# Hybrid decoder block on one core: the second half of the tokens gathered in three 8-bit parts for the first pair of experts, and the sorting of the experts behind it

## The chip, the cores and the metric

The kernel runs on one NeuronCore of one Trainium2 chip. The metric is the time of one execution on the device in microseconds (us). The kernel before takes 444.64 us, the median of 3 runs (443.95 to 445.56).

## What is computed

A decoder block over 272 tokens (16 learned meta tokens and 256 of the input) of width 1024: a normalisation, one projection whose columns feed two mixers (a state-space mixer and a gated short convolution), a product with the output weights, a residual sum, and a mixture of experts, all in float32. The part that the change touches is the last one:

```python
p_group = softmax(t @ wg_r + bg_r)
g_val, g_idx = top_k(p_group, 1)
...
top_v, top_i = top_k(sel, TOP_K)
top_w = softmax(top_v)
...
for e in range(N_EXPERTS):
    h = silu(t @ w_gate[e]) * (t @ w_up[e])
    out = out + combine[:, e:e + 1] * (h @ w_down[e])
```

Each of 256 tokens picks one group of four experts and two experts in it. There are 16 experts, each with three float32 matrices of 1024 x 512, about 100 MB of weights in all.

## The kernel before, in words

**Stages.** The projection, the mixers and the output product fill the first 225 us. Then the router chooses experts, and a loop goes over `UNITS`: six pairs of experts, then one group of four. `side_by_side` puts a pair's two products next to each other in the array, 64 columns each; so a pair can hold at most 64 tokens of each expert, which is checked at the end (`rv > CAP`).

**Tokens to slots.** The tokens lie in `hh`, two halves (b = 0 and 1) of 128 tokens by 1024 values, each row scaled. `rk` holds the rank of a token among those of an expert; `pick` makes of it a 0/1 matrix `P` (token by slot), and a product with `P` gathers an expert's tokens, already turned, into the PSUM tile `xp`. `rows` (VectorE) multiplies `xp` by a column of weights and writes `X`, the moving operand's partner in the products `gu` (gate, then up). For the first pair `gather` (line 900) uses float32 `hh` and float32 `P`. For the later pairs `gather3` (line 1110) uses bf16: each float32 value is split into three bf16 parts of 8 bits each, `hparts[j][b]`, with three products per block and half. The parts are made by ScalarE (`Copy` to bf16) and VectorE (subtraction) after the first `X`, at lines 1099 to 1108, while TensorE does the first pair's `gu`.

**Router and sorting.** `ranks(b)` needs the choice of half b; the second half's ranks also count the first half's tokens. `sort_experts` (line 876, 15 small VectorE instructions) sorts ten of the experts by their number of tokens (the first `FIXED` = 6 stay where they are): `order` says which expert stands at which place, `mosti` is the largest count, `rk` is put in order. `weights` (line 997) makes the tokens' weights of their experts, `cparts`.

**Sequencer numbers.** `values_load` (line 1176) lets every engine's sequencer read `mosti` into a register (`TENSOR_LOAD`), which only the branch at the end needs. Line 1177 lets SyncE's queue (SP) read `order` into ten registers, which the loads of weights of the sorted experts need.

**Weights.** All weights come by DMAs of 1 MB, issued in order by SP (line 113) into a ring of 22 slots plus 3 more (`RING2`), 25 tiles in all. A tile's slot is freed when TensorE has read it (`used`, called after every fourth block of `gu` and every second of `yd`), and the next load into it is issued then. A pair takes 12 tiles: 4 gate, 4 up, 4 down. `fin`, a 512 KB copy of the last normalisation's weights to all partitions, is loaded at line 774, in the middle of the projection.

**A pair.** `gu` gate (8 blocks), `gu` up (8 blocks), then `back` (line 1031: products `ptp` with `P` and `cparts`), `gather3` of the next pair in two pieces with the turning `hbp` of the hidden values between them, then `yd` (down), whose results are scattered to the accumulators `acc` during the next pair's `gu`.

```python
for kind in range(2):
    g = bank("pj", "gu")
    for k in range(KT):
        side_by_side(g, Xf, w_of(u, kind, k, 0, 512), k, k == 0, k == KT - 1)
        if k % 4 == 3:
            used(ne)
```

Of the kernel before, what the change touches and what calls it, by code (L numbers as in the profile page):

```python
# [39 lines left out]
def body(ctx, tc, x, meta_tokens, norm_mix, w_in, ssd_conv_w, ssd_conv_b, dt_bias, A_log, D_skip,  # L40
# [95 lines left out]

    fin = cp.tile([128, D], F32, name="fin")
    lg = cp.tile([128, 2, 20], F32, name="lg")
# [601 lines left out]
    for i, (name, j, c, t0) in enumerate(units):  # L740
        hold(i)
        if name[0] == "c" and c == 0:
            cc = v["cc" + name[1]]
        split_hi(i + 2)
        if i == B + 1:
            split_hi(i + 3)
        for f, a in pre.get(i, []):
            f(*a)
        if name == "o":
            if c == 0:  # L750
                second(i - 1)
            split_lo(i + 2)
            if c < 14:
                for b in range(2):
                    out_product(i, b)
        else:
            p = project(i)
            split_lo(i + 2)
            if i in (0, 1):
                x_part(i, 1 - i)  # L760
            if i == B + 1:
                first(i, p)
            if i:
                second(i - 1)
            if i != B + 1:
                first(i, p)
        fill(i)
        if i == NU - 1 and dbg is not None and "yn" in dbg:
            nc.sync.dma_start(dbg["yn"][:, 0:2048], v["y", 0].rearrange("p t l -> p (t l)"))
        if i == NU - 1:  # L770
            eu.close()
            right = ctx.enter_context(tc.tile_pool(name="ring2", bufs=RING2, side="right"))
            load(RING2, right)
            nc.sync.dma_start(fin, raw(norm_final, 0, [[0, 128], [1, D]]))
    if dbg is not None and "yn" in dbg:
# [73 lines left out]
    def ranks(b):  # L849

        p = rp[:, 64 + 16 * b:80 + 16 * b]
        T.matmul(p, sup, mem[:, b], start=True, stop=(b == 0))
        if b:
            T.matmul(p, onesb, mem[:, 0], start=False, stop=True)
        V.scalar_tensor_tensor(rk[:, b, 0:NE], mem[:, b], -1024.0, p, op0=OP.mult, op1=OP.add)

# [18 lines left out]

    def sort_experts(counts):
        m, key = NE - FIXED, place
        t = small("srt", 2 * m * m)
        c = counts[:, FIXED:NE]
# [20 lines left out]
    def gather(b, q, p, i0=0, i1=4):  # L900

        for i in range(i0, i1):
            T.matmul(p[:, i], hh[:, b].rearrange("p (m k) -> p k m", k=KT)[:, 4 * q + i],  # L903
                     P[:, b], start=(b == 0 and i == 0), stop=(b == 1),
                     skip_group_check=True)

# [55 lines left out]
    busy(1)  # L962
    P = bp.tile([128, 2, 128], F32, name="P")
    pick(P, 0, 0)
# [3 lines left out]
    xp = [bank(tag, "xp").rearrange("p (k t) -> p k t", k=4) for tag in ("pj", "m")]  # L968
    gather(0, 0, xp[0])
    for i in range(4):  # L970
        places(1, i)
    gather(0, 1, xp[1], 0, 1)
    ranks(1)
    gather(0, 1, xp[1], 1, 4)
    pick(P, 0, 1)

# [5 lines left out]
    mosti = cp.tile([128, 1], I32, name="mosti")  # L982
    sort_experts(rp[:, 96:112])
    for q in range(2):
        gather(1, q, xp[q])
    es.close()
# [97 lines left out]

    h3 = wk.tile([128, 2, D], BF, name="h3")
    tm = wk.tile([128, S], F32, name="tm", tag="PT")
    X = wk.tile([128, KT, 128], F32, name="X")
    for q in range(2):
        rows(X, xp[q], q)
    weights(tm)  # L1090
    ws0 = wk.tile([128, 1], F32, name="ws", tag="ws")
    P = wk.tile([128, 2, 128], BF, name="P", bufs=2)
    for b in range(2):
        pick(P, 0, b)


    hb0, hb1 = (hh[:, b].bitcast(BF).rearrange("p (j d) -> p j d", j=2) for b in range(2))
    hparts = [[h3[:, 0], hb0[:, 0]], [h3[:, 1], hb0[:, 1]], [hb1[:, 0], hb1[:, 1]]]
    rem = [wk.tile([128, 512], F32R, name="rem", tag=t).bitcast(BF) for t in ("Yh", "Yl")]
# [29 lines left out]
    def over():  # L1129
# [45 lines left out]

    rv = nc.values_load(mosti[0:1], min_val=0, max_val=2 * S)
    chosen += nc.values_load_multi_w_load_instructions(
        order[0:1], engines=[mybir.EngineType.SP], min_val=FIXED, max_val=NE - 1,
        skip_runtime_bounds_check_because="a sum of one of the numbers FIXED to NE - 1 and of zeros")[1]
    left = {}  # L1180
    s3 = wk.tile([128, 2], F32, name="s3")
    s4 = wk.tile([128, 2, 2], F32, name="s4")
    for u, ne in enumerate(UNITS):
# [19 lines left out]
        if last:  # L1203

            A.activation(s3[:, 0:1], eps, AF.Sqrt)
            hd = turned(hb)
        PT, ws = back(P, cparts[:, :, places_of(u)])
        if not last:
# [105 lines left out]
```

## Time and profile before

| | |
|---|---|
| median of 3 runs | 444.64 us |
| the profiled execution | 445.38 us |
| span of the profiled execution, first to last instruction | 443.4 us |
| TensorE matmul busy | 423.8 us (96%) |
| TensorE weight load busy | 295.0 us (67%) |
| VectorE, ScalarE, GpSimd busy | 220.3, 159.0, 89.1 us |
| mean granted TensorE clock | 0.989 |
| HBM read | 138.26 MB |

Times inside the profile count from the first instruction. PE is TensorE's matmuls and PEld its weight loads, DVE is VectorE, ACT ScalarE, SPq SyncE's queue, which issues the DMAs; PEldq, DVEq and so on are the sequencers. `L1050` is line 1050. In a timeline row stand the start, the time taken, engine, line, operation, the tiles, shapes and a count, and in brackets how long the engine was idle before and who released it. A float32 product of the program shows as two matmul records.

### The profile page before, as it was taken

The page shows a single profiled execution, that of the slowest core. Times are in us where ns is not written, and L with a number is a line of the kernel's source. Part 1 is how long each engine was busy: PE and PEld are TensorE (multiplying, and loading weights), DVE is VectorE, ACT ScalarE, POOL GpSimd, SP SyncE. Part 2 cuts the span into 40 slices and gives each one's busy share as a digit, 9 for nine tenths or more (in the row PEclk, how much of TensorE's full clock was granted, in tenths as well). Part 3 has the DMA queues.
Part 4 walks back from the last instruction along what each step waited for, and adds up shares of the span by engine and source line. Part 5 has one row for each costly group of instructions (what it writes and reads, how often), then busy time and mean ns, then how long its engine had stood idle before and what let it go on. Part 6 is the DMA issues. An engine that isn't in the chain of part 4 may idle for free.

```text
span 443.4 us, 7446 instructions
## 1 busy us (share of the span) xinstructions
PE 423.8 (96%) x2923; PEld 295.0 (67%) x2923; DVE 220.3 (50%) x465; ACT 159.0 (36%) x247; POOL 89.1 (20%) x113
## 2 busy tenths in 40 slices
PE   8899999899999899999999999999999999999982
PEld 5799999799998899888877363533535335353241
DVE  7769888758795768695557521110212102121013
ACT  6766346645757344744472401010010100101121
POOL 2345334854668154000000000000000000000000
PEclk9999999999999999999999989999999999999997
DMA  8997977066699566599692999999999999999952
GB/s 232 342 312 250 348 250 266 32 191 188 194 360 413 182 209 233 199 407 419 199 362 102 370 400 375 425 418 424 419 421 421 422 418 420 421 418 422 412 224 98
DMA packets 48892, 139.85 MB, mean 315 GB/s; under 512 B 6342, under 2 KB 32342, under 8 KB 36822
## 3 DMA queue, kind: packets, MB, share of 16 engines
q1 hardware_dynamic: 47990, 138.22, 82.5%
q10 hardware_dynamic: 864, 1.12, 0.7%
q8 instruction: 25, 0.41, 0.4%
q14 instruction: 13, 0.11, 0.1%
HBM read 138.26 MB, written 1.06 MB: 314 GB/s over the span
## 4 chain that ended last, share of the span: by engine, by line
PE 64%; DVE 7%; ACT 3%; issue 2%; POOL 1%; DVEq 0%; ACTq 0%
PE gu L1050 22%; PE yd L1050 11%; PE acc L347 10%; PE xp L1115 4%; PE p_c L339 3%; PE acc L1071 3%; PE p_h L339 3%; PE p_b L339 3%; ACT f L310 1%; PE hbp L1057 1%; DVE h L619 1%; PE xp L903 1%; DVE f L326 1%; POOL f L324 1%; DVE h L548 1%
## 5 line engine op out<-in xcount | busy, mean ns | idle before, releaser
L1050 PE MATMUL gu<-w,X 128*64 128x512 f32 (+1 forms) x512 | 100.0, 595 | 0.4 <-DVE X L1082 0.4
L324 POOL TENSOR_TENSOR f<-w,f 128x256 fp32r<-128x256 f32 x96 | 82.6, 892 | 87.5 <-ACT f L310 77.7
L310 ACT ACTIVATE f<-w 128x1024 fp32r<-128x1024 f32 x64 | 67.1, 1054 | 35.9 <-POOL f L324 12.6
L1050 PEld LDWEIGHTS gu<-w,X 128*64 128x64 f32 (+1 forms) x512 | 31.3, 130 | 61.2 <-issue 59.5
L326 DVE TENSOR_TENSOR f<-w,f 128x1024 fp32r<-128x1024 f32 x40 | 50.6, 1264 | 17.4 <-ACT f L310 17.4
L1050 PE MATMUL yd<-w,hd 128*64 128x512 f32 (+2 forms) x288 | 50.9, 548 | 0.5 <-DVE hd L1060 0.5
L347 PE MATMUL acc<-f,h 128*128 128x512 f32 x192 | 44.8, 391 | 0.0
L1202 DVE TENSOR_TENSOR hb<-hb,gu 128x512 f32<-128x512 f32 x7 | 4.8, 688 | 74.0 <-PE gu L1050 71.9
L347 PEld LDWEIGHTS acc<-f,h 128*128 128x128 f32 x192 | 35.5, 188 | 7.7 <-issue 0.4
L1065 ACT ACTIVATE Yh<-yd,ws 128x512 fp32r<-128x512 f32 x13 | 8.9, 688 | 79.2 <-PE yd L1050 62.5
L1050 PEld LDWEIGHTS yd<-w,hd 128*64 128x64 f32 (+1 forms) x288 | 16.7, 128 | 29.3 <-issue 25.5
L1066 DVE SCALAR_TENSOR_TENSOR Yl<-yd,ws,Yh 128x512 fp32r<-128x512 f32 x12 | 9.0, 751 | 53.6 <-PE yd L1050 38.5
L1115 PE MATMUL xp<-P,hh 128*128 128x128 bf16 x192 | 20.1, 232 | 0.0
L1115 PEld LDWEIGHTS <-hh 128*128 128x128 bf16 x192 | 18.8, 149 | 1.6 <-issue 1.6
L1115 PE MATMUL xp<-P,h 128*128 128x128 bf16 x96 | 17.7, 235 | 1.6 <-ACT hb L1196 1.6
L339 PE MATMUL p_z<-uh,f 128*128 128x256 f32 x128 | 17.3, 285 | 1.9 <-POOL f L324 1.9
L339 PE MATMUL p_c<-uh,f 128*128 128x258 f32 x128 | 16.8, 283 | 1.3 <-DVE h L607 1.3
L339 PE MATMUL p_xs<-uh,f 128*128 128x272 f32 x128 | 18.0, 292 | 0.0
L1196 ACT ACTIVATE hb<-gu 128x512 f32<-128x512 f32 x7 | 4.2, 594 | 37.0 <-PE gu L1050 37.0
L339 PEld LDWEIGHTS p_z<-uh,f 128*128 128x128 f32 x128 | 15.6, 188 | 2.4 <-POOL f L324 2.3
L339 PE MATMUL p_b<-uh,f 128*128 128x256 f32 x128 | 16.6, 281 | 0.7 <-DVE h L607 0.7
L1042 ACT ACTIVATE PT<-ptp 128x256 fp32r<-128x256 f32 x7 | 2.7, 385 | 39.7 <-PE ptp L1038 39.7
(331 smaller groups left out, 648.5 us busy)
## 6 DMA issues: line engine op xcount, KB each, us to landing
w<-in_expert_w_gate SPq DMA_DIRECT2D x32, 1024.0 KB, 11.7
w<-in_expert_w_up SPq DMA_DIRECT2D x32, 1024.0 KB, 14.5
w<-in_expert_w_down SPq DMA_DIRECT2D x28, 1024.0 KB, 13.6
w<-in_w_in SPq DMA_DIRECT2D x23, 1024.0 KB, 7.2
w<-in_w_out SPq DMA_DIRECT2D x8, 1024.0 KB, 9.4
abc<-adr SPq DMA_DIRECT2D x2, 1024.0 KB
w<-in_expert_w_down SPq DMA_DIRECT2D x4, 512.0 KB
w<-in_expert_w_down SPq DMA_DIRECT2D x8, 256.0 KB, 10.5
```

Source lines behind the costliest of these rows:

```text
L310: A.activation(h, src, AF.Copy)
L324: G.tensor_tensor(l[:, k:k + 2], src[:, k:k + 2], h[:, k:k + 2].bitcast(F32), op=OP.subtract)
L326: V.tensor_tensor(l, src, h.bitcast(F32), op=OP.subtract)
L339: T.matmul(p, st_[:, k, :], mv[:, k, t0:], start=(k == 0 and st_ is terms[0][0] and mv is uh), stop=(k == KT - 1 and mv is ul))
L347: T.matmul(acc[b][n], st_[:, 128 * b:128 * (b + 1)], mv[:, 512 * n:512 * (n + 1)], start=False, stop=False, skip_group_check=True)
L548: V.tensor_tensor(yt(4 * hf, 4), yt(4 * hf, 4), v["zs"][:, 4 * hf:4 * hf + 4], op=OP.mult)
L1050: T.matmul(o[c * s:c * s + c], X[:, 128 * k + c * s:128 * k + c * s + c], ws_, start=first_, stop=last_, tile_position=(0, c * s))
L1065: A.activation(Yh, y, AF.Copy, scale=ws)
L1066: V.scalar_tensor_tensor(Yl, y, ws, Yh.bitcast(F32), op0=OP.mult, op1=OP.subtract)
L1071: T.matmul(acc[b][n], PT[:, 128 * b:128 * (b + 1)], part, start=False, stop=stop and part is Y[-1], skip_group_check=True)
L1115: T.matmul(p[:, i], hparts[j][b].rearrange("p (m k) -> p k m", k=KT)[:, 4 * q + i], P[:, b], start=(j == b == 0), stop=(j == 2 and b == 1))
L1202: V.tensor_mul(hb, hb, g)
```

## The change

- The first pair's gather of the second half of the tokens is made with three bf16 parts (24 products) and no longer in float32 (8 products, 16 records). So the second half's parts are made before the first `X`, on ScalarE and VectorE, while TensorE gathers the first half.
- `sort_experts` moves from before the first `X` to behind it, and behind the making of the first half's parts.
- The reading of `order` by SP moves into the loop, behind the first pair's `gu`. The reading of `mosti` by all sequencers moves to the end of the second pair.
- `fin` is loaded after the router, before the first refill of the ring, and no longer in the projection. `h3` (two of the second half's parts) takes its place in memory.

```diff
-            nc.sync.dma_start(fin, raw(norm_final, 0, [[0, 128], [1, D]]))
...
         if b:
             T.matmul(p, onesb, mem[:, 0], start=False, stop=True)
+            return
...
-    gather(0, 0, xp[0])
+    gather(0, 0, xp[0], 0, 3)
     for i in range(4):
         places(1, i)
-    gather(0, 1, xp[1], 0, 1)
     ranks(1)
-    gather(0, 1, xp[1], 1, 4)
-    pick(P, 0, 1)
+    P1 = bp.tile([128, 2, 128], BF, name="P1")
+    A.activation(h3[:, 0], hh[:, 1], AF.Copy)
+    V.tensor_tensor(hh[:, 1], hh[:, 1], h3[:, 0], op=OP.subtract)
+    A.activation(h3[:, 1], hh[:, 1], AF.Copy)
+    V.scalar_tensor_tensor(rk[:, 1, 0:NE], mem[:, 1], -1024.0, rp[:, 80:96], op0=OP.mult, op1=OP.add)
+    pick(P1, 0, 1)
+    rem1 = hh[:, 1].bitcast(BF)[:, 0:D]
+    V.tensor_tensor(rem1, hh[:, 1], h3[:, 1], op=OP.subtract)
+    gather(0, 0, xp[0], 3, 4)
+    gather(0, 1, xp[1])
...
-    sort_experts(rp[:, 96:112])
-    for q in range(2):
-        gather(1, q, xp[q])
+    for js in ((0, 1), (2,)):
+        for k in range(KT):
+            for j in js:
+                T.matmul(xp[k // 4][:, k % 4], (h3[:, 0], h3[:, 1], rem1)[j].rearrange("p (m k) -> p k m", k=KT)[:, k],
+                         P1[:, 1], start=False, stop=(j == 2), skip_group_check=True)
...
+    fin = wk.tile([128, D], F32, name="fin")
+    nc.sync.dma_start(fin, raw(norm_final, 0, [[0, 128], [1, D]]))
...
     for q in range(2):
         rows(X, xp[q], q)
+    hb0, hb1 = (hh[:, b].bitcast(BF).rearrange("p (j d) -> p j d", j=2) for b in range(2))
+    hparts = [[hb1[:, 1], h3[:, 0]], [hb0[:, 1], h3[:, 1]], [hb0[:, 0], rem1]]
+    rem = wk.tile([128, 512], F32R, name="rem", tag="Yh").bitcast(BF)
+    A.activation(hparts[0][0], hh[:, 0], AF.Copy)
+    V.tensor_tensor(hh[:, 0], hh[:, 0], hparts[0][0], op=OP.subtract)
+    A.activation(rem, hh[:, 0], AF.Copy)
+    V.tensor_tensor(hparts[2][0], hh[:, 0], rem, op=OP.subtract)
+    A.activation(hparts[1][0], rem, AF.Copy)
+    sort_experts(rp[:, 96:112], sorting)
     weights(tm)
...
-    for b in range(2):
-        A.activation(hparts[0][b], hh[:, b], AF.Copy)
-        if b == 0:
-            A.activation(ws0, eps, AF.Silu)
-        V.tensor_tensor(hh[:, b], hh[:, b], hparts[0][b], op=OP.subtract)
-        A.activation(hparts[1][b], hh[:, b], AF.Copy)
-        V.tensor_tensor(rem[b], hh[:, b], hparts[1][b], op=OP.subtract)
-    for b in range(2):
-        A.activation(hparts[2][b], rem[b], AF.Copy)
...
-    rv = nc.values_load(mosti[0:1], min_val=0, max_val=2 * S)
-    chosen += nc.values_load_multi_w_load_instructions(
...
+        if u == 0:
+            chosen += nc.values_load_multi_w_load_instructions(
...
+        if u == 1:
+            rv = nc.values_load(mosti[0:1], min_val=0, max_val=2 * S)
```

On VectorE, from the second half's choice (`mem`) to the first pair's slots, the order before was as follows (the rows of the sorting, `place` to `mosti`, and of the weights, `tm` to `cparts`, are left out where "..." stands):

```order
L846 SCALAR_TENSOR_TENSOR mem<-cnt 128x16
...
L898 TENSOR_TENSOR mosti<-most,srt 128x1
L1082 TENSOR_TENSOR X<-xp,gf 128x512 x2
L1003 TENSOR_REDUCE tm<-lg 128x10
...
L865 TENSOR_TENSOR P<-sl,rk 128x128 x2
L1104 TENSOR_TENSOR hh<-hh,h_2725 128x1024
L1106 TENSOR_TENSOR rem<-hh,h_2725 128x1024
L1104 TENSOR_TENSOR hh<-hh 128x1024
L1106 TENSOR_TENSOR rem<-hh 128x1024
L1176 TENSOR_LOAD mosti
L865 TENSOR_TENSOR P<-sl,rk 128x128 x2
```

The same place on VectorE in the changed kernel:

```order
L1091 TENSOR_TENSOR X<-xp,gf 128x512 x2
L1106 TENSOR_TENSOR hh<-hh 128x1024
L1108 TENSOR_TENSOR hh<-hh,rem 128x1024
...
L898 TENSOR_TENSOR mosti<-most,sorting 128x1
L1012 TENSOR_REDUCE tm<-lg 128x10
...
L1030 CAST cparts<-comb 128x52
L866 TENSOR_TENSOR P<-sl,rk 128x128 x4
L1206 TENSOR_TENSOR hb<-hb,gu 128x512
```

The sorting stood ahead of `X` and now stands behind it; two of the four large subtractions went ahead of `X`, and the four 0/1 matrices of the first and second pair come last.

On SP's queue the loads around the first pair were issued in this order before:

```order
L113 DMA w_2606<-in_expert_w_down 128x2048
L1176 TENSOR_LOAD mosti
L1176 ISA x2
L1177 TENSOR_LOAD order
L113 DMA w_2814<-in_expert_w_gate 128x2048
```

And in the changed kernel, where `w_2793` is the first refill, `w_2837` the eighth and `w_2942` the ninth:

```order
L113 DMA w_2605<-in_expert_w_down 128x2048
L1096 DMA fin<-in_norm_final 128x1024
L113 DMA w_2793<-in_expert_w_gate 128x2048
...
L113 DMA w_2837<-in_expert_w_up 128x2048
L1212 TENSOR_LOAD order
L113 DMA w_2942<-in_expert_w_down 128x2048
```

The two readings of numbers no longer stand ahead of the first refill; `fin` does.

## Rows read from the trace of the kernel before

**Rows 1.** The page, busy time of each engine.
```profile
PE 423.8 (96%) x2923; PEld 295.0 (67%) x2923; DVE 220.3 (50%) x465; ACT 159.0 (36%) x247; POOL 89.1 (20%) x113
```
**Rows 2.** Windows: PE, PEld, DVE, ACT, POOL busy, PEclk, DMA share, GB/s.
```profile
272.00:426.00 154.00, 152.55 (x971) 64.21 (x970) 25.17 (x48) 14.26 (x24) 0.00 (x0) 1.00 1.01 419
426.00:429.00 3.00, 3.00 (x42) 1.48 (x35) 0.64 (x1) 0.69 (x1) 0.00 (x0) 1.00 0.55 201
```
**Rows 3.** Timeline of TensorE's weight loads in the last group's down product.
```profile
426.56 1.86 PEld L1050 LDWEIGHTS yd<-w,hd 128*32 128x32 f32 x30 [0.47 <-DMA w<-in_expert_w_down]
428.63 0.14 PEld L1050 LDWEIGHTS yd<-w,hd 128*32 128x32 f32 x2 [0.22 <-DMA w<-in_expert_w_down]
```
**Rows 4.** Windows around the first pair, columns as in Rows 2.
```profile
235.50:243.50 8.00, 7.61 (x34) 5.32 (x36) 7.08 (x33) 2.67 (x4) 0.00 (x0) 1.00 0.01 4
246.00:265.00 19.00, 17.35 (x115) 9.52 (x113) 7.08 (x11) 5.94 (x7) 0.00 (x0) 0.91 1.01 423
265.00:272.00 7.00, 7.00 (x34) 2.45 (x30) 1.52 (x3) 1.37 (x2) 0.00 (x0) 1.00 0.93 309
```
**Rows 5.** Timeline of SP's queue, the first and third refills of the ring.
```profile
243.45 4.24 SPq L113 DMA_DIRECT2D w<-in_expert_w_gate  x4
...
264.45 4.43 SPq L113 DMA_DIRECT2D w<-in_expert_w_down  x4
```
**Rows 6.** Timeline, from the router's end to the first product.
```profile
228.77 2.34 ACT L813 ACTIVATE hh<-hh,rsh 128x1024 f32<-128x1024 f32 x2
...
235.34 4.07 PE L903 MATMUL xp<-P,hh 128*128 128x128 f32 x16
235.52 0.17 DVE L880 SCALAR_TENSOR_TENSOR place<-rp,count 128x10 f32<-128x10 f32 x1 [1.07 <-PE rp L980]
...
238.90 0.16 DVE L898 TENSOR_TENSOR mosti<-most,srt 128x1 int32<-128x1 f32 x1
238.98 1.28 DVE L1082 TENSOR_TENSOR X<-xp,gf 128x512 f32<-128x512 f32 x2
...
239.80 13.95 PE L1050 MATMUL gu<-w,X 128*64 128x512 f32 x64 [0.39 <-DVE X L1082]
```
**Rows 7.** The chain of waits, first and second pair: start, us, engine, tile.
```profile
253.76 0.22 PE ptp L1035 x2
...
254.21 1.04 ACT hh L1108
...
255.79 2.34 PE xp L1115 x24
...
260.84 7.02 PE yd L1050 x32
...
284.14 0.22 PE ptp L1035 x2
...
286.70 1.48 PE xp L1115 x24
288.18 7.02 PE yd L1050 x32
```
**Rows 8.** Windows: the clock after that stall, columns as in Rows 2.
```profile
256.00:260.00 4.00, 4.00 (x42) 3.95 (x40) 1.91 (x4) 0.01 (x1) 0.00 (x0) 0.57 1.01 418
```
**Rows 9.** Timeline, one part of a half, the weights, the slots, a table load.
```profile
231.13 1.28 ACT L977 ACT_TABLE_LOAD   x1
...
240.18 0.18 DVE L1003 TENSOR_REDUCE tm<-lg 128x10 f32<-128x40 f32 x1
...
244.54 0.49 DVE L865 TENSOR_TENSOR P<-sl,rk 128x128 bf16<-128x128 f32 x2
...
246.20 1.06 ACT L1105 ACTIVATE h<-hh 128x1024 bf16<-128x1024 f32 x1 [2.88 <-DVE hh L1104]
...
247.29 1.23 DVE L1106 TENSOR_TENSOR rem<-hh,h 128x1024 bf16<-128x1024 f32 x1 [1.12 <-ACT h L1105]
```
**Rows 10.** Line 1176: the sequencers' reading of `mosti`, min/median/max ns, first and last start.
```profile
L1176 PEldq TENSOR_LOAD <-mosti x1: 492/492/492, 239.1 to 239.1; - x1
```

More of the change, by code (lines that the diff above doesn't have):

```diff
@@ L135, in body @@
     order = cp.tile([128, NE - FIXED], I32, name="order")
-    fin = cp.tile([128, D], F32, name="fin")
+    h3 = cp.tile([128, 2, D], BF, name="h3")
     lg = cp.tile([128, 2, 20], F32, name="lg")
@@ L874, in in_order, with sort_experts @@
         V.tensor_reduce(out_, t, axis=AX.X, op=OP.add)
-    def sort_experts(counts):
+    def sort_experts(counts, t):
         m, key = NE - FIXED, place
-        t = small("srt", 2 * m * m)
         c = counts[:, FIXED:NE]
@@ L903, in gather @@
             T.matmul(p[:, i], hh[:, b].rearrange("p (m k) -> p k m", k=KT)[:, 4 * q + i],
-                     P[:, b], start=(b == 0 and i == 0), stop=(b == 1),
-                     skip_group_check=True)
+                     P[:, b], start=(i == 0), stop=False, skip_group_check=True)
     def busy(n):
@@ L962, in body @@
     busy(1)
-    P = bp.tile([128, 2, 128], F32, name="P")
+    P = bp.tile([128, 1, 128], F32, name="P")
     pick(P, 0, 0)
@@ L1083, in rows @@
                         op=OP.mult)
-    h3 = wk.tile([128, 2, D], BF, name="h3")
+    fin = wk.tile([128, D], F32, name="fin")
+    nc.sync.dma_start(fin, raw(norm_final, 0, [[0, 128], [1, D]]))
     tm = wk.tile([128, S], F32, name="tm", tag="PT")
@@ L1089, in body @@
         rows(X, xp[q], q)
+    hb0, hb1 = (hh[:, b].bitcast(BF).rearrange("p (j d) -> p j d", j=2) for b in range(2))
[7 more added lines that the diff above has]
+    sort_experts(rp[:, 96:112], sorting)
     weights(tm)
     ws0 = wk.tile([128, 1], F32, name="ws", tag="ws")
+    A.activation(ws0, eps, AF.Silu)
     P = wk.tile([128, 2, 128], BF, name="P", bufs=2)
@@ L1094, in body @@
         pick(P, 0, b)
-    hb0, hb1 = (hh[:, b].bitcast(BF).rearrange("p (j d) -> p j d", j=2) for b in range(2))
-    hparts = [[h3[:, 0], hb0[:, 0]], [h3[:, 1], hb0[:, 1]], [hb1[:, 0], hb1[:, 1]]]
-    rem = [wk.tile([128, 512], F32R, name="rem", tag=t).bitcast(BF) for t in ("Yh", "Yl")]
-    for b in range(2):
-        A.activation(hparts[0][b], hh[:, b], AF.Copy)
-        if b == 0:
-            A.activation(ws0, eps, AF.Silu)
-        V.tensor_tensor(hh[:, b], hh[:, b], hparts[0][b], op=OP.subtract)
-        A.activation(hparts[1][b], hh[:, b], AF.Copy)
-        V.tensor_tensor(rem[b], hh[:, b], hparts[1][b], op=OP.subtract)
-    for b in range(2):
-        A.activation(hparts[2][b], rem[b], AF.Copy)
     def gather3(P, X, q):
@@ L1174, in over @@
                         scatter(b, n, PTo, Yo)
-    rv = nc.values_load(mosti[0:1], min_val=0, max_val=2 * S)
-    chosen += nc.values_load_multi_w_load_instructions(
-        order[0:1], engines=[mybir.EngineType.SP], min_val=FIXED, max_val=NE - 1,
-        skip_runtime_bounds_check_because="a sum of one of the numbers FIXED to NE - 1 and of zeros")[1]
     left = {}
@@ L1206, in body @@
             hd = turned(hb)
+        if u == 0:
+            chosen += nc.values_load_multi_w_load_instructions(
+                order[0:1], engines=[mybir.EngineType.SP], min_val=FIXED, max_val=NE - 1,
+                skip_runtime_bounds_check_because="a sum of one of the numbers FIXED to NE - 1 and of zeros")[1]
         PT, ws = back(P, cparts[:, :, places_of(u)])
```

## The prediction

> **What bounds the kernel now.** I read the busy times first, then the windows by stage, then the last group's weight loads, and only then the stretch that the change touches. [...] The windows tell more: in the 154 us from 272 to 426 the DMA engines have a busy share of 1.01 and move 419 GB/s without a break, and the stream ends at about 428.6 [rows 2]. At the very end TensorE's weight loads of the last down product wait for exactly these loads, at 426.56 and again at 428.63 [rows 3]. So from 272 on the stream of weights sets the end, with TensorE just ahead of it. Its bytes are fixed; its end can only move by its start and by the holes in it.
>
> Both can be seen. From 235.5 to 243.5 the DMA engines move almost nothing, 4 GB/s: all 25 slots of the ring are full and the first slot comes free only when TensorE is half through the first gate product. A second, shallow hole is the window 265 to 272 with 309 GB/s; before it, from 246 to 265, the rate is 423 [rows 4]. The refills show why: the first is issued at 243.45, which is 3.65 us after the first product begins at 239.80 [rows 5, 6], and the third only at 264.45, when the loads issued before have run out [rows 5]. [...]
>
> **Term 1: the first product begins earlier.** Before, TensorE comes to the second half's gather at 235.34 and takes 16 records, 4.07 us, to 239.41. VectorE meanwhile sorts from 235.52 to 239.06 and begins the first `X` at 238.98, although its bank was complete when half the gather was done; the first product follows 0.82 us later, at 239.80 [rows 6]. The change takes the sorting out of this path and shortens the gather. The first half's gather, the ranks and the counts stay ahead in the same number, so TensorE still reaches the second half at 235.34. There it has 24 bf16 records; the same form takes 1.48 us in a later pair [rows 7]. `X`'s first piece needs 20 of them: 20/24 x 1.48 = 1.23 us and some 0.2 for the last to end, 236.8.
>
> The parts must be ready by then. ScalarE ends the scaling at 231.11 (228.77 + 2.34) [rows 6]; then follow a conversion of 1.06, a subtraction of 1.23, a conversion of 1.06 and a subtraction of 1.23 [rows 9], with about 0.03 us at each hand-over and 0.2 for VectorE's compares, which stand before: 235.9 in all. The products of the third part begin at 235.34 + 16/24 x 1.48 = 236.3. So the split is covered by the first half's gather, with 0.4 us to spare; if that cover were gone, each further microsecond would move `X` one for one. `X` at 236.85, the first product at 236.85 + 0.82 = 237.67: **2.1 us earlier**. [...] The trace has 1.48/24 = 62 ns for this very form, and I go by it. Bounds: if these 24 records run as slowly as the first such gather now does, 2.34 us at the low clock [rows 7], 20 of them take 1.95 and the gain is 1.4; if nothing but the third part binds (235.9, four products and `X`), it is 2.5. I take 2.1, since the clock of this stretch was 1.00 throughout. TensorE's idle time before the first product grows from 0.39 to about 0.7 us, far less than the 1.6 us behind which the clock fell.
>
> The first refill hangs on the first product by 3.65 us and so is issued at about 241.3. The whole stream starts 2.1 us earlier.
>
> **Term 2: the first pair's stall.** From the last up product to the first down product the first pair takes 260.84 - 253.76 = 7.08 us, the second 288.18 - 284.14 = 4.04 [rows 7]. The difference of 3.04 is the wait for ScalarE and the low clock behind it. In the change only the first half's parts are made behind `X`: three conversions and two subtractions. On VectorE, from `X` at 236.85: two pieces 1.28 [rows 6], subtraction 1.23, wait for ScalarE 1.1, subtraction 1.23 [rows 9], the sorting 3.54 (235.52 to 239.06) [rows 6], the weights 4.48 (240.18 to 244.66), slots of the first pair 0.49 [rows 9]: 250.2; the second pair's slots 250.7. TensorE ends its products at 237.67 + 13.95 = 251.6 [rows 6]. That leaves 1.4 us, so the stall goes, and with it the low clock. ScalarE has a table load (1.28) [rows 9] and small work between, done by about 248, while the hidden values are needed at 251.6. What is late next is nothing in this pair; the down product begins at 237.67 + (260.84 - 239.80) - 3.04 = 255.7.
>
> The third refill follows it by 3.61 us (264.45 - 260.84) [rows 5, 7], at about 259.3, while the stream, 2.1 us ahead of before, has work until 263. The shallow hole closes: (419 - 309) x 7 / 419 = **1.8 us**. Bounds: 0 if the stall remains, 1.8 if it goes. I take the upper end, by the margin just worked out.
>
> **Small edits.** `fin`, 0.52 MB, moves into the empty stretch from 235.5 on and needs 1.25 us at 419 GB/s; it waits for the memory of router tiles, last read by the gather at about 237, and is through before 241.3. If it were later it would cost up to 1.25 us of the stream. The reading of `order` stands behind the eighth refill on SP, when the sorting is over by 8 us, and the next refill is due only at 259.3: nothing. The reading of `mosti` takes TensorE's sequencer 0.49 us [rows 10], now between two products of the second pair. Bounds 0 and 0.49; I take 0 for the end, since TensorE then is 2.1 + 3.0 - 3.9 = 1.2 us further ahead of the stream than now.
>
> **Sum.** 2.1 + 1.8 = 3.9 us off the end of the stream; the tail behind it is as before. The profiled execution (445.38, of which 443.4 span) would go to 441.5; it lies 0.74 above the median of the runs, so from the median 444.64 the forecast is **440.7 us**.
>
> **Rivals.**
> - TensorE, not the stream, sets the end: then both its gains count in full, 2.1 + 3.0 = 5.1 us, 439.5 us. For it speaks the 96% [rows 1]; against it the share of 1.01 and the waits for DMA at the end [rows 2, 3]. [...]
> - Only the first term pays: VectorE or ScalarE is late for the first pair, or the clock falls in the longer idle time before the first product, and the hole stays: 2.1 us, 442.5; with `fin` in the stream's way besides 1.25 less, 443.8.
> - The change does not do what it says, since the extra split sits on the path (third part 1.7 us late) and the stall stays at `back`: gain under 0.4 us, 444.3.
> - It is slower: the chain on VectorE behind `X` grew by the sorting. Its margin is 1.4 us. Beyond that, TensorE stalls in `back`, and a stall brings back the low clock (3.04 - 1.6 = 1.4 us). TensorE's gain is then 5.1 - 1.4 - stall, so the kernel is slower than before once the stall is over 3.7 us, that is if VectorE's chain of 13.4 us took 18.5. At 20 us, the stall is 5.2: 446.1 us. Every operation of it has a row now, so this would need waits that no row shows.
>
> **How the numbers follow.** The forecast's case has a chance of 0.58, TensorE at the end 0.12, the first term alone 0.16, no visible effect 0.08, slower 0.06. A measurement of this kernel can tell about 0.3%, 1.33 us, from no change, so the third case with `fin` in the way counts as no change in part. Faster 0.84, same 0.10, slower 0.06. The range reaches from TensorE at the end (439.5, less 0.3 for the upper bound of term 1) to the first term alone (442.5) with 0.5 for the spread of the runs: 439.2 to 443.0.
>
> **What would show it.** In the changed profile: the first `gu` product at 237.4 to 238.0 and the sorting behind `X`; the first refill of the ring near 241.3; the clock at 1.00 from 230 to 300; some 4.0 us between the first pair's last up and first down product; the third refill near 259.3 and no window under 400 GB/s between 246 and 420; the last loads landing near 424.7, with the weight loads of the last down product waiting longer for DMA than now. I am wrong if `X` begins after 237.5, if TensorE waits for VectorE at `back`, or if the stream ends earlier and the kernel does not.

## The result and the profile after

The changed kernel takes **442.41 us**, the median of 20 runs (440.77 to 444.33); the kernel before, on the same chip, 445.59 (20 runs, 443.39 to 447.29). The ratio is 0.9933, with a 95% interval of 0.9918 to 0.9949: 3.2 us faster. From the 444.64 that the prediction started from it said 3.9 us less, 440.7, with a range of 439.2 to 443.0.

The profiled execution took 442.56 us, span 440.5, mean granted clock 0.990. The busy line of the page, which answers to [rows 1]:

```profile
PE 422.1 (96%) x2931; PEld 291.1 (66%) x2931; DVE 219.9 (50%) x465; ACT 158.1 (36%) x246; POOL 89.2 (20%) x113
```

It tells nothing new, as before. The timeline of the changed kernel does, from the first half's gather to the first pair's down product; the columns are start, time taken, engine, line, operation, and the idle time before with who ended it:

```profile
232.36 1.67 PE L903 MATMUL xp<-P,hh 128*128 128x128 f32 x6 [0.24 <-ACT hh L813]
...
235.69 1.23 DVE L980 TENSOR_TENSOR hh<-hh,h 128x1024 bf16<-128x1024 f32 x1 [0.71 <-ACT h L976]
...
236.45 1.17 PE L993 MATMUL xp<-P,h 128*128 128x128 bf16 x16
...
237.46 0.64 PE L993 MATMUL xp<-P,hh 128*128 128x128 bf16 x8
237.90 1.29 DVE L1091 TENSOR_TENSOR X<-xp,gf 128x512 f32<-128x512 f32 x2 [0.98 <-PE xp L993]
...
238.65 13.95 PE L1059 MATMUL gu<-w,X 128*64 128x512 f32 x64 [0.54 <-DVE X L1091]
...
242.32 4.24 SPq L113 DMA_DIRECT2D w<-in_expert_w_gate  x4
...
242.64 0.17 DVE L880 SCALAR_TENSOR_TENSOR place<-rp,count 128x10 f32<-128x10 f32 x1
...
246.02 0.16 DVE L898 TENSOR_TENSOR mosti<-most,sorting 128x1 int32<-128x1 f32 x1
...
250.46 0.89 DVE L866 TENSOR_TENSOR P<-sl,rk 128x128 bf16<-128x128 f32 x4
...
252.53 0.29 PE L1044 MATMUL ptp<-idt,P 128*128 128x128 bf16 x2
...
256.55 4.94 PE L1059 MATMUL yd<-w,hd 128*64 128x512 f32 x22
...
260.23 4.24 SPq L113 DMA_DIRECT2D w<-in_expert_w_down  x4
```

The second half's gather is 24 bf16 products in 1.65 us where it was 4.07, `X` follows it at once, and the sorting runs from 242.64 to 246.18, behind `X`, while TensorE is in its first product. The slots of the first pair are there by 251, before TensorE ends the up product at 252.5, so it goes straight on: 4.02 us from `ptp` to the down product, where it took 7.08 [rows 7].

The windows of the changed kernel (busy time of each engine, granted clock, share and rate of the DMA engines), which answer to [rows 2, 4]; the first three lines are in the projection:

```profile
86.00:88.00 2.00, 1.56 (x10) 1.53 (x10) 0.00 (x0) 1.06 (x1) 0.83 (x2) 0.82 0.00 0
88.00:90.00 2.00, 2.00 (x16) 1.43 (x16) 0.00 (x0) 1.33 (x2) 2.00 (x4) 0.50 0.25 48
90.00:92.00 2.00, 2.00 (x19) 1.59 (x18) 0.78 (x2) 0.00 (x0) 0.34 (x1) 0.82 0.95 309
...
256.00:258.00 2.00, 2.00 (x19) 1.08 (x18) 0.69 (x1) 0.00 (x0) 0.00 (x0) 1.00 0.97 397
...
265.00:272.00 7.00, 7.00 (x30) 2.75 (x30) 1.15 (x3) 0.69 (x1) 0.00 (x0) 1.00 1.00 415
272.00:424.00 152.00, 150.55 (x963) 63.27 (x963) 24.80 (x46) 14.26 (x24) 0.00 (x0) 1.00 1.01 418
424.00:427.00 3.00, 2.70 (x32) 1.18 (x24) 0.75 (x1) 0.69 (x1) 0.00 (x0) 1.00 0.30 105
```

The clock behind the first pair's up product is 1.00, the shallow hole has closed (415 GB/s from 265 to 272, where it was 309), and the stream runs at 418 until about 424.8 (3 us at 105 in the last window are 0.75 us at 418). But in the projection, far ahead of everything that the change touches, the clock fell to 0.50 in this execution, behind a wait of 1.89 us for GpSimd. In the profile of before the same wait, 1.90 us, was followed by full clock:

```profile
88.00:90.00 2.00, 2.00 (x28) 1.56 (x27) 0.00 (x0) 1.33 (x2) 1.98 (x3) 1.00 0.23 30
```

So the first half's gather began 1.10 us later here, at 232.36; before, its row was

```profile
231.26 2.62 PE L903 MATMUL xp<-P,hh 128*128 128x128 f32 x10 [0.24 <-DVE P L865]
```

The span is still 2.9 us shorter: counted from that gather the end came 4.0 us earlier. The end itself, TensorE's weight loads in the last group's down product, which answer to [rows 3]:

```profile
421.53 0.33 PEld L1059 LDWEIGHTS yd<-w,hd 128*32 128x32 f32 x2 [0.51 <-DMA w<-in_expert_w_down]
...
422.88 0.14 PEld L1059 LDWEIGHTS yd<-w,hd 128*32 128x32 f32 x2 [0.54 <-DMA w<-in_expert_w_down]
423.55 1.86 PEld L1059 LDWEIGHTS yd<-w,hd 128*32 128x32 f32 x30 [0.54 <-DMA w<-in_expert_w_down]
425.61 0.14 PEld L1059 LDWEIGHTS yd<-w,hd 128*32 128x32 f32 x2 [0.20 <-DMA w<-in_expert_w_down]
```

The last of these waits is at 425.61, where it was at 428.63. Six of TensorE's weight-load rows in this product name a DMA, where four did before: TensorE is further ahead of the stream.

### The profile page after: what moved, and what is told of

The parts are those of the page before. It is cut to its first block, busy times and chain, and to the rows that moved or that the text cites. A ratio compares the mean times of both kernels' runs of the same rounds, so it can differ in the third digit from the quotient of the medians.

```text
span 440.5 us, 7463 instructions
## 1 busy us (share of the span) xinstructions
PE 422.1 (96%) x2931; PEld 291.1 (66%) x2931; DVE 219.9 (50%) x465; ACT 158.1 (36%) x246; POOL 89.2 (20%) x113
## 5 line engine op out<-in xcount | busy, mean ns | idle before, releaser
L1059 PEld LDWEIGHTS gu<-w,X 128*64 128x64 f32 (+1 forms) x512 | 30.4, 130 | 62.2 <-issue 60.6
L1059 PE MATMUL yd<-w,hd 128*64 128x512 f32 (+2 forms) x288 | 52.2, 548 | 0.8 <-DVE hd L1069 0.5
L340 PE MATMUL p_h<-uh,f 128*128 128x258 f32 x128 | 16.8, 284 | 0.0
```

Of the source, the lines that this page charges most:

```text
L340: T.matmul(p, st_[:, k, :], mv[:, k, t0:], start=(k == 0 and st_ is terms[0][0] and mv is uh), stop=(k == KT - 1 and mv is ul))
L1059: T.matmul(o[c * s:c * s + c], X[:, 128 * k + c * s:128 * k + c * s + c], ws_, start=first_, stop=last_, tile_position=(0, c * s))
```

## The experiments

Theory: the stream of weights sets the end; the change starts it earlier (term 1) and closes its hole behind the first pair (term 2). Rivals: TensorE sets the end; only term 1 pays; what looks like the change is a clock that falls in one profile and not in another. Besides medians I give spans by how often the clock fell; a fall is a stretch in which the granted clock goes down to 0.50 of full speed and comes back, as from 88 to 90 above. One fall costs the mean clock 0.004: in the changed kernel's profile the three windows from 86 to 92 lose 2 x (0.18 + 0.50 + 0.18) = 1.7 us of 440. In the tail behind the last weights the clock falls once more in both profiles of each kernel and in those of the first two kernels with extra products below (its mean from 430 to 440 is 0.71 to 0.86; the 0.73 in the repeat of the change costs the mean of the whole 0.006); that fall is not counted here. The mean clocks of all executions lie near 0.994, 0.990 and 0.986, which I read as no fall before the tail, one, and two. The tail's fall is not always of the same length, so the bounds between these groups are not sharp, and where a fall lay is known only for the profiled executions.

### The two kernels once more

No edit.

> The kernel before once more, to see the granted clock of many executions. Theory 'chance in the projection' (in some executions of either kernel the clock falls to its lower level behind the wait of 1.9 us for GpSimd at 84.5 to 86.4 us, which cost 1.5 us in the profiled execution of the changed kernel and did not happen in that of the kernel before): the mean granted clock of its executions falls in two groups some 0.004 apart, about as often as in the changed kernel, and the ratio to itself is 1.000 +- 0.002. Rival 'the change slows the projection': the executions of the kernel before show one group only.

445.87 us against 445.88 in the other runs of before, ratio 1.0004 (0.9985 to 1.0023). What it gave is its profile. The stall in the first pair is there as before (`ptp` at 252.41, the down product at 258.08), but the clock did not fall behind it, and the hole all but vanished. Windows of this second profile of the kernel before:

```profile
256.00:258.00 2.00, 2.00 (x31) 2.00 (x28) 1.29 (x2) 0.00 (x0) 0.00 (x0) 1.00 1.02 426
...
262.00:275.00 13.00, 13.00 (x60) 4.75 (x58) 1.90 (x4) 1.71 (x3) 0.00 (x0) 1.00 1.01 412
```

The interval from `ptp` to the down product is 5.67 us where it was 7.08 [rows 7], the clock of 256 to 258 is 1.00 where it was 0.57 from 256 to 260 [rows 8], and 412 GB/s against 420 leaves a hole of 13 x 8/420 = 0.25 us, not 1.8. The mean clock was 0.995, the span 441.1.

> The changed kernel on the same chip as the next two, so that they can be compared. 442.4 us, 3.0 to 3.2 us under the kernel before; clocks of 0.993 in half of the executions and 0.989 to 0.990 in the others.

441.91 us (6 runs), ratio 0.9925 (0.9895 to 0.9954); in this profile the clock fell nowhere before the tail, span 439.6. All executions of both kernels in this study, grouped by mean clock (median span, in brackets how many):

```
mean granted clock     0.993 and more   0.988 to 0.992   0.987 and less
before                 441.8 (14)       443.8 (39)       444.7 (39)
changed                439.75 (14)      441.35 (12)      - (0)
```

Two things follow. At the same number of falls the change gains 2.05 and 2.45 us. And it has fewer falls: (39 + 2 x 39)/92 = 1.27 an execution before, 12/26 = 0.46 after. No execution of the changed kernel shows two. My theory, falls in the projection alone and about as often in either kernel, was wrong: the kernel before has a second place where the clock falls.

### Does the stream or TensorE set the end?

Two extra products of 128x512, 1.7 us, ahead of the first pair's gate product, or of the fourth pair's (`u == 3`):

```diff
+            if u == 0 and kind == 0:
+                for i in range(2):
+                    T.matmul(g, Xf[:, 0:128], w_of(u, 0, 0, 0, 512)[0], start=True, stop=True)
```

> Two extra float32 products of 128 x 512 on TensorE (0.86 us each by the rows of the same shape, 1.7 us in all) ahead of the first pair's first product; they leave the result as it is. Theory 'stream' (the end follows the start of the refills and their holes): the first refill comes 1.7 us later and so does the end, 444.1 us. Theory 'TensorE sets the end': also 1.7 us later, 444.1 us. Neither is told apart here; it is the measure for the next run.

443.96 us, ratio 0.9973 (0.9953 to 0.9993), 2.05 over the repeat of the change. By the groups above, the span with no fall is 441.75 (8 executions), 2.0 over the changed kernel's 439.75, and with one 442.25 (4), 0.9 over its 441.35. Three of the eight, at a clock of 0.993 and spans of 442.8 to 443.5, may have had a fall; the other five, at 0.995 and 0.996, give 441.5, which is 1.75 over. Delaying the stream's start costs about its length, though the executions with a fall show less.

> The same two products ahead of the fourth pair's first product. Theory 'stream': the DMA engines have some five loads queued there and do not notice, and TensorE has over 2 us to spare before the last loads land: 442.4 us, +-0.4 of the changed kernel. Theory 'TensorE sets the end': 1.7 us later, 444.1 us.

443.01 us, ratio 0.9938 (0.9919 to 0.9958). The median is 1.1 over the repeat of the change, but 8 of its 12 executions had a fall and only 2 of 6 there. At equal falls: 439.7 against 439.75 with none (4 executions), 441.5 against 441.35 with one (8). The same work some 80 us later costs nothing, so TensorE does not set the end.

Third, 4 products (3.4 us) between the first pair's up and down product, so that TensorE is late there but never idle:

```diff
+        if u == 0:
+            gx = bank("pj", "gx")
+            for i in range(4):
+                T.matmul(gx, Xf[:, 0:128], w_of(u, 2, 0, 0, 512)[0], start=True, stop=True)
```

> The changed kernel with 4 more products of 128x512 (3.4 us by the 0.85 us of one such product) between the up and the down product of the first pair: a stall of the length of before's, and more, but with TensorE busy, so that the clock has no reason to fall. If the stream of weights sets the end: the third refill comes 3.4 us later behind the first (17.9 + 3.4 = 21.3 us); about 1.5 us of it are slack, since the stream has transfers queued until then, so a hole of 1.5 to 2.2 us opens at 265 to 270 and the time is 443.4 to 444.1 us. If TensorE sets the end: +3.4 us, 445.3 us. If a delay behind the first product costs nothing at all (term 2 was empty even in the profile of before): 441.9 us.

444.14 us, ratio 0.9969 (0.9947 to 0.9991); with no fall 441.9 (7 executions), 2.15 over the change, and with one 442.9 (5), 1.55 over, as the stream theory has it, not 3.4. In its profile the clock was 1.00 in every window from 250 to 280, the third refill was issued 21.4 us behind the first (17.9 in the repeat of the change), and a hole opened. SP's queue and windows of this kernel:

```profile
241.46 4.24 SPq L113 DMA_DIRECT2D w<-in_expert_w_gate  x4
...
262.88 4.24 SPq L113 DMA_DIRECT2D w<-in_expert_w_down  x4
```

```profile
262.00:266.00 4.00, 4.00 (x20) 1.29 (x18) 0.00 (x0) 0.52 (x1) 0.00 (x0) 1.00 0.78 254
266.00:272.00 6.00, 6.00 (x26) 2.26 (x22) 1.90 (x4) 0.85 (x2) 0.00 (x0) 1.00 1.01 425
```

4 x (1 - 254/420) = 1.6 us of hole. So a delay of TensorE at this place has some 1.3 to 1.9 us of slack (3.5 us of delay less 2.15 or 1.6) and costs what exceeds it; this is the mechanism of term 2, alone and without the clock.

### Is the clock behind the stall what the second term was made of?

The kernel before, with two products more in the first pair's `back`, so that TensorE waits for ScalarE a shorter time, while the parts come no sooner:

```diff
-    def back(P, cm):
+    def back(P, cm, fill=0):
...
+        for i in range(fill):
+            T.matmul(p, idt, w_of(0, 2, 0, 0, 512)[0], start=True, stop=True)
...
-        PT, ws = back(P, cparts[:, :, places_of(u)])
+        PT, ws = back(P, cparts[:, :, places_of(u)], 2 * (u == 0))
```

> The kernel before with two float32 products of 128 x 512 (1.7 us) on TensorE where it waits 1.6 us for ScalarE in the first pair; they leave the result as it is. Theory 'the hole comes from the clock' (the clock falls behind this wait in some 7 of 10 executions of the kernel before, and only then does the third refill come so late that the stream of weights has a hole of 1.8 us; the wait alone leaves 0.2): the clock stays at 1.00 behind the wait, the mean clock never is under 0.988, and the median falls by 0.7 x 1.3 = 0.9 us to 445.0; the changed kernel then gains only 2.1 us over it, what the first product gains. Rival 'the hole comes from the wait itself': the hole stays and the median is that of the kernel before, 445.9.

445.42 us, ratio 0.9985 (0.9957 to 1.0013): 1.0 below the median of before on that chip, 446.45, but the interval holds no change. The clocks tell more: none of its 12 executions is at 0.987 or less, against 15 of 25 of the kernel before on the same chip. On that chip the kernel before had 1.44 falls an execution, this one 8 in 12, that is 0.67. So one of the two falls stood behind this stall, in most executions; the other, seen in its profile from 87 to 92 (0.66), is the projection's. Behind the first pair its profile shows full clock and no hole:

```profile
254.00:262.00 8.00, 8.00 (x74) 5.16 (x72) 3.62 (x8) 2.87 (x4) 0.00 (x0) 1.00 1.01 423
262.00:270.00 8.00, 8.00 (x38) 2.77 (x35) 0.75 (x1) 0.69 (x1) 0.00 (x0) 1.00 1.02 416
```

At equal falls it is no faster than the kernel before: 442.5 (4) against 441.8, and 443.95 (8) against 443.8. The changed kernel is 2.75 and 2.6 ahead of it, somewhat more than the 2.1 that I expected.

### The two halves of term 1

The changed kernel with the sorting ahead of `X` again:

```diff
+    sort_experts(rp[:, 96:112], small("srt", 2 * (NE - FIXED) ** 2))
...
-    sort_experts(rp[:, 96:112], sorting)
```

> The changed kernel with only the sorting put back ahead of X; the gather by parts, the late reading of numbers and the rest stay. By the rows of the changed kernel VectorE is done with the third part at 236.9 and X begins at 237.9; with 3.5 us of sorting behind the third part X begins at 240.5. Theory 'the first product sets the stream's start': 2.6 us later, 445.0 us, no better than 0.9 us under the kernel before. Rival 'the shorter gather on TensorE is what pays': within 0.5 us of the changed kernel.

446.73 us, ratio 1.0015 (0.9984 to 1.0045): no gain is left. Timeline of this kernel:

```profile
237.28 1.19 PE L994 MATMUL xp<-P,h 128*128 128x128 bf16 x16
237.66 0.16 DVE L880 SCALAR_TENSOR_TENSOR place<-rp,count 128x10 f32<-128x10 f32 x1
...
238.30 0.65 PE L994 MATMUL xp<-P,hh 128*128 128x128 bf16 x8
...
241.03 0.16 DVE L898 TENSOR_TENSOR mosti<-most,srt 128x1 int32<-128x1 f32 x1
241.11 1.28 DVE L1092 TENSOR_TENSOR X<-xp,gf 128x512 f32<-128x512 f32 x2
...
241.84 1.61 PE L1060 MATMUL gu<-w,X 128*64 128x512 f32 x4 [2.89 <-DVE X L1092]
```

The gather is done by 239 and TensorE idles 2.89 us for the sorting. Behind this wait the clock fell as well, to 0.57 and 0.58 in the two windows from 242 to 246, and the first 64 records took 15.65 us in place of 13.95: the 1.7 us above the expected 445.0. At equal falls the span is 442.3 (1 execution) and 443.8 (3), 2.55 and 2.45 over the changed kernel, which is the delay of 2.6 that the theory gave.

The other half: sorting behind `X`, but the float32 gather back, and all parts cut behind `X`, in this kernel behind the sorting and the first pair's slots too:

```diff
...
-    P1 = bp.tile([128, 2, 128], BF, name="P1")
-    A.activation(h3[:, 0], hh[:, 1], AF.Copy)
-    V.tensor_tensor(hh[:, 1], hh[:, 1], h3[:, 0], op=OP.subtract)
-    A.activation(h3[:, 1], hh[:, 1], AF.Copy)
...
-    pick(P1, 0, 1)
-    rem1 = hh[:, 1].bitcast(BF)[:, 0:D]
-    V.tensor_tensor(rem1, hh[:, 1], h3[:, 1], op=OP.subtract)
+    pick(P, 0, 1)
...
+    for q in range(2):
+        gather(1, q, xp[q])
...
+    for b in range(2):
+        A.activation(hparts[0][b], hh[:, b], AF.Copy)
...
+        V.tensor_tensor(hh[:, b], hh[:, b], hparts[0][b], op=OP.subtract)
```

> The changed kernel with the second half of the tokens gathered in float32 again, and all parts cut behind X as before; sorting stays behind X. It separates the two halves of term 1. Before X the gather of the second half is 8 float32 products and X waits for nothing of the three 8-bit parts. In the profile of before the float32 gather was done in time and X was late because of sorting, so if the sorting was all of term 1, X comes as early as in the change or up to 1.2 us earlier (no cutting ahead of it), and the first product begins 5 to 6.3 us behind the start of the gather. My theory: that is so, but the cutting of both halves now stands behind X on VectorE, and sorting behind that, so P for the first pair is late by the length of the second half's cutting; from VectorE's rows that is a stall of 4 to 6 us between the up and the down product of the first pair in place of none, the hole in the stream of weights returns with 2 to 4 us, and the time is 444 to 447 us. Rival (cutting was free on the other engines): no stall, time as the change, 441.9 us or a little less.

449.56 us, ratio 1.0082 (1.0051 to 1.0114): slower than before, by more than I expected. Timeline and windows of this kernel:

```profile
235.53 4.07 PE L903 MATMUL xp<-P,hh 128*128 128x128 f32 x16
237.71 0.69 DVE L1083 TENSOR_TENSOR X<-xp,gf 128x512 f32<-128x512 f32 x1 [4.04 <-PE xp L903]
...
239.53 13.95 PE L1051 MATMUL gu<-w,X 128*64 128x512 f32 x64
...
248.06 0.49 DVE L866 TENSOR_TENSOR P<-sl,rk 128x128 bf16<-128x128 f32 x2
...
253.41 0.29 PE L1036 MATMUL ptp<-idt,P 128*128 128x128 bf16 x2
...
259.41 0.26 PE L1118 MATMUL xp<-P,h 128*128 128x128 bf16 x1 [5.55 <-ACT hb L1195]
```

```profile
258.00:260.00 2.00, 0.59 (x6) 0.59 (x6) 0.61 (x2) 1.64 (x3) 0.00 (x0) 0.50 1.01 418
...
264.00:272.00 8.00, 8.00 (x49) 3.27 (x49) 0.69 (x1) 0.69 (x1) 0.00 (x0) 1.00 0.48 164
```

I was wrong about the first product here. The first piece of `X` did come earlier than before, 6.27 us behind the start of the gather (before 7.72, changed 5.54), but the product cannot start before the gather itself ends, at about 239.5; I had counted only `X`. The stall of 5.55 us came in the length that I expected, but not for my reason: I had the slots `P` late. The sorting stood ahead of the cutting, the slots were there by 248.6 and `ptp` ran on time at 253.41; TensorE waited for the parts, whose last two conversions ScalarE did from 256.87 to 258.87. The clock fell during the stall, and the hole is 8 x (1 - 164/420) = 4.9 us. With the first product 1.8 us later than in the change that is 6.7 of the 7.7 us by which its span exceeds 439.75; the gather began 0.2 us later than in the repeat of the change, and the rest, 0.7, I cannot place.

The time from the first half's gather to the first product, in the four kernels:

```
                     sorting ahead of X     sorting behind X
float32 gather       8.54 (before)          8.09
three bf16 parts     8.65                   6.29 (changed)
```

Each half alone is worth 0.45 and -0.11 us, both together 2.25. Either the sorting or the float32 gather is enough to hold the first product.

### The small edits

Both readings of sorted numbers put back ahead of the loop:

```diff
+    rv = nc.values_load(mosti[0:1], min_val=0, max_val=2 * S)
+    chosen += nc.values_load_multi_w_load_instructions(
...
-        if u == 0:
-            chosen += nc.values_load_multi_w_load_instructions(
...
-        if u == 1:
-            rv = nc.values_load(mosti[0:1], min_val=0, max_val=2 * S)
```

> The changed kernel with both readings of the sorted numbers (mosti by every engine, order by SyncE's queue) put back ahead of the loop over pairs, as they stood in the kernel before, while sorting stays behind X. Theory: every sequencer then waits for the end of sorting before it may go on; sorting ended 7.6 us behind the first product's start in the profile of the change (246.2 against 238.65), so TensorE's first product begins about 8 us later, the first refill of the stream too, and the time is 441.9 + 8 = 449 to 451 us. Rival (the reading only keeps the sequencer that needs the number, TensorE's first product goes on): 442 us, no change.

453.20 us, ratio 1.017 (1.0123 to 1.0218). Timeline of this kernel:

```profile
247.50 15.66 PE L1059 MATMUL gu<-w,X 128*64 128x512 f32 x64 [8.81 <-DVE tm L1016]
```

The first product begins 14.56 us behind the gather's start, 8.3 later than in the change, and takes 1.7 us more, since the clock fell in the idle time (0.54 from 240 to 250, 0.88 from 250 to 254); the median lies 2.2 us over the 449 to 451 that I expected, and this is 1.7 of it. SP's queue waited 8.1 us at the reading of `mosti` (L1184), and TensorE's product, which stands behind its own reading of it, 8.81. This profile has the projection's fall too, and its gather began 1.7 us later than in the repeat of the change: 11.7 of the 12 us by which its span, 451.7, exceeds 439.75. Sorting can stand behind `X` only if TensorE's sequencer does not wait for its numbers; what SP's reading alone would cost was not run.

`fin` loaded in the projection again:

```diff
+    fin = cp.tile([128, D], F32, name="fin")
...
+            nc.sync.dma_start(fin, raw(norm_final, 0, [[0, 128], [1, D]]))
...
-    fin = wk.tile([128, D], F32, name="fin")
-    nc.sync.dma_start(fin, raw(norm_final, 0, [[0, 128], [1, D]]))
```

> The changed kernel with the load of fin put back in the projection, where it stood before. Theory: in the change it goes out in the empty stretch ahead of the first refill, so its place is worth nothing: 441.9 us, within 0.5 us of the change. Rival: its 0.5 MB take their place in the stream of weights, 1.2 us at 420 GB/s, so putting it back gains 1.2 us: 440.7 us.

443.47 us, ratio 0.9943 (0.9921 to 0.9964). There is no gain, so the rival falls; but the median is 1.6 above the repeat of the change, three times the 0.5 that I allowed. At equal falls it is 441.45 (10) against 441.35, and 440.25 (2) against 439.75. Ten of its 12 executions had a fall, against 12 of 26. The place of the load is not the cause: it was issued at 186.65 in this profile (184.4 in that of before), some 95 us behind the fall at 88 to 94, and near the end of the first 225 us rather than in the middle. On the same chip the kernel of `delay_back`, without this load in the projection, had 5 of 12; why this one had more stays open.

### A version that goes further

The projection's wait of 1.9 us filled with 14 products whose result is not used:

```diff
+        if i == at["z0", 3]:
+            for k in range(14):
+                T.matmul(p, wh[:, k % KT, :], uh[:, k % KT, t0:], start=True, stop=True)
```

> The changed kernel with 14 extra products of 128 x 256 (1.7 us) on TensorE in the projection where it waits 1.9 us for GpSimd at 84.5 us; they leave the result as it is. Theory 'chance in the projection': the clock no longer falls there, the mean clock is 0.993 or more in every execution, and the slower group (441.4 us of span against 439.7) is gone: median 441.7 us against 442.4. Rival 'the two groups come from something else': the groups stay.

442.24 us, ratio 0.9912 (0.9883 to 0.994). That is not the 441.7 that I expected, and the slower group is not gone: of 9 executions 7 had no fall (span 439.9; one of them, at 0.993 and 441.1, is not certain) and 2 had one (441.8). The profiled one was of the two, with clock 1.00 in the projection and a fall at a third place. Windows of this kernel:

```profile
234.00:236.00 2.00, 2.00 (x11) 1.94 (x11) 1.25 (x4) 1.92 (x2) 0.00 (x0) 0.73 0.96 406
236.00:238.00 2.00, 2.00 (x22) 2.00 (x21) 0.38 (x1) 1.57 (x3) 0.00 (x0) 0.50 0.08 29
```

In addition, 0.79 MB of tile 25 loaded while the stream stands empty, into 6 KB a partition that `fin` then leaves free, with `fin` at the very end:

```diff
+                if j == NW + 25:
+                    nc.sync.dma_start(w[:, 1536:2048], rows_[:, 1536:2048])
...
-    fin = wk.tile([128, D], F32, name="fin")
-    nc.sync.dma_start(fin, raw(norm_final, 0, [[0, 128], [1, D]]))
+    ring3 = ctx.enter_context(tc.tile_pool(name="ring3", bufs=1, side="right"))
+    early = ring3.tile([128, 1536], F32, name="early")
+    nc.sync.dma_start(early, raw(expert_w_gate, experts_at[25][0] * D * 512, [[4096, 128], [1, 1536]]))
...
+    fin = slot("fin", free.pop(0))[:, 0:1024]
+    nc.sync.dma_start(fin, raw(norm_final, 0, [[0, 128], [1, D]]))
```

> The same, and three quarters of one more weight tile (0.79 MB) loaded in the stretch in which the DMA engines stand still before the first refill, into 6 KB per partition that are free there once the last norm's weights are loaded at the very end, into a freed slot. Theory 'stream': 0.79 MB less behind the first refill, 1.9 us at 419 GB/s; TensorE has 2.2 us to spare before the last loads: 1.9 us under 'filled', 439.8 us. Theory 'TensorE sets the end': no gain over 'filled'.

441.11 us (6 runs), ratio 0.9896 (0.9855 to 0.9936), the best of the study; its interval overlaps that of the change. All 6 executions are without a fall, span 439.1, 0.65 under the changed kernel's 439.75 and 0.8 under the filled kernel's 439.9, not the 1.9 that I expected. The bytes are worth 0.79/0.419 = 1.9 us; part of it was given back at once: the stream now has less to load before the third refill, and that refill, at 258.47, comes too late for it. Windows of this kernel:

```profile
260.00:265.00 5.00, 5.00 (x24) 1.87 (x22) 0.75 (x1) 1.16 (x2) 0.00 (x0) 1.00 0.97 365
```

5 x (1 - 365/420) = 0.65 us of new hole. The first product also began 6.53 us behind the first half's gather, 0.24 later than in the change. The rest, some 0.2 us, I cannot place; `fin`, issued at 419.63, now runs beside the last weights. In the two filled kernels together 2 of 15 executions had a fall, against 12 of 26 of the changed kernel.

## Why the prediction was right, and where not

**What bounds the kernel: right.** 1.7 us of extra work ahead of the first product cost 0.9 to 2.0 us by the groups of falls, the same work ahead of the fourth pair nothing. The 96% did not tell this: from 272 to 424 TensorE's matmuls were busy 150.55 of 152 us and its weight loads 63.27, and in that stretch the extra work of the fourth pair found room.

**Term 1: right, 2.25 us for 2.1.** `X` began 5.54 us behind the first half's gather (5.59 forecast) and the first product 6.29 behind it (6.41). The bf16 records ran (237.46 - 236.45)/16 = 63 ns apart, where I took 62 from the later pair. The split stayed covered: its last subtraction ended at 236.92, the products that need it began at 237.46. What I had not seen is that sorting alone was worth next to nothing: the float32 gather ended at 239.41, 0.4 us ahead of the first product, and would have held it.

**Term 2: the mechanism right, the size not.** In the changed kernel everything came as worked out: 4.02 us from `ptp` to the down product (4.0), the third refill 21.58 us behind the first product (21.6), no hole (415 GB/s from 265 to 272). The step that failed is "I take the upper end": I sized the hole, 1.8 us, from one execution of the kernel before in which the clock had fallen behind the stall. The stall, 1.65 and 1.64 us in which TensorE waits for ScalarE ahead of the next gather, is in both profiles of that kernel, the fall in one (0.57 from 256 to 260 [rows 8], against 1.00). Without it the hole measured 0.25 us, because the stream has some 1.5 us of slack there (1.3 to 1.9 by the third delay). With no fall before the tail the change is worth 2.05 us (the two profiles' terms would make 2.25 + 0.25), not 3.9. The rest is that it takes away the stall behind which the clock fell in most executions: 0.81 falls fewer an execution, close to the 0.77 that the held kernel lost when only that stall was filled. With the changed kernel's shares (14 and 12 of 26) the spans of before in the table would average 442.7 in place of 443.9, so the falls are worth 1.2 us; with 2.05 and 2.45 at equal falls that makes 3.4, against 3.2 measured (2.3 to 3.7 by its interval). So term 2 pays, by this estimate, 3.4 - 2.25 = 1.1 us on average, inside its bounds of 0 and 1.8.

**Small edits: right.** `fin` went out at 238.18, ahead of the first refill at 242.32, and its old place is no better. The reading of `mosti`, 505 ns, left no gap on TensorE; that of `order` at 253.5 was done long before the third refill at 260.23.

**Sum.** Between the two profiled executions the forecast fits better than it deserves: 4.0 us from the first half's gather on, since the profile of before had the fall behind the stall and not the one in the projection. Against the median, 442.41 lies 1.7 us above the 440.7: 0.95 of it is the start, since the three runs of before that I had gave 444.64 and the 20 gave 445.59, and 0.7 the gain, 3.2 for 3.9.

**Rivals.** TensorE at the end would give 439.5; the fourth-pair run excludes it. The first term alone, 442.5, is nearest to the median, but by its lower start: from 445.59 it would be 443.5 and the forecast 441.7, which is nearer. As a mechanism it is what remains where the clock does not fall. That the split sits on the path, or VectorE's chain behind `X` stalls `back`, did not happen. The float32 kernel had a stall of 5.55 us, over the 3.7 from which the kernel was to be slower than before, and was slower; but it lacks 1.8 us of term 1 as well, so it does not test that bound.

## What to carry to other kernels

A term that contains a low clock should be sized from several executions, not one (the hole measured 1.8 us in one profile of before and 0.25 in the other): look at the mean granted clock of every run before calling a slow stretch a property of the kernel. Where two things hold the same start, taking away either may be worth next to nothing (0.45 and -0.11 us here), so price them together. And where a stream of loads sets the end, as here, an engine's delay counted only by what exceeded the loads already queued: 3.5 us of it between the first pair's products cost 2.15.

## What the hardware showed that I had not expected

The same wait gave different clocks. In twelve profiles TensorE waited 1.89 or 1.90 us for GpSimd in the projection; the clock fell behind it in five and stayed at 1.00 in seven. Two kernels of the study side by side, the repeat of the change and the one with `fin` put back:

```profile
88.00:90.00 2.00, 2.00 (x28) 1.55 (x27) 0.00 (x0) 1.33 (x2) 1.98 (x3) 1.00 0.19 38
```

```profile
88.00:90.00 2.00, 2.00 (x14) 1.59 (x15) 0.00 (x0) 1.35 (x3) 1.18 (x2) 0.69 0.00 0
90.00:92.00 2.00, 2.00 (x18) 1.42 (x17) 0.00 (x0) 0.72 (x1) 1.60 (x3) 0.50 0.63 142
```

Behind the first pair's 1.6 us stall it fell in one profile of before and not in the other. In the filled kernel it fell from 234 to 238 (0.73 and 0.50) with no wait above 0.3 us on TensorE in the 5 us before. In or behind waits of 2.89, 5.55 and 8.81 us it fell in the one profile that there is of each (lowest window 0.57, 0.50 and 0.54). What decides it for the short ones these runs do not show.
